# A gated merge on one core: banks given out by last read, sums finished early, new orders of the gate products, x read back in eight steps

## The chip, the core and the metric

The kernel runs on one core of a Trainium2 chip. The metric is the device time of one execution in microseconds. Engines: PE (matrix products, with PEld loading its weights), DVE (elementwise), ACT (copies, casts, activations), POOL, and SP (here it only issues DMAs). Each has a queue of its own and takes its instructions in order; they wait for one another by semaphores. PE writes into eight accumulator banks, each 128 x 512 in f32.

## The reference

One layer of a hybrid decoder on x of 256 x 2048, in f32. The part that the change touches:

```python
z = x @ mix_w_in[i]
b_gate, c_gate, h_conv, q_raw, f_raw, i_in, g_raw, gate_conv, gate_hgrn = jnp.split(z, splits, axis=-1)
y_conv = short_conv_mixer(b_gate, c_gate, h_conv, conv_w[i])
y_hgrn = hgrn2_mixer(q_raw, f_raw, i_in, g_raw, lower_bounds[i], hg_norm_w[i])
merged = (jax.nn.sigmoid(gate_conv) * (y_conv @ branch_w_conv[i])
          + jax.nn.sigmoid(gate_hgrn) * (y_hgrn @ branch_w_hgrn[i]))
x = layer_norm(ALPHA * x + merged @ mix_w_out[i], ln_g[i, 1], ln_b[i, 1])
```

gate_conv and gate_hgrn are 2048 columns each; y_conv and y_hgrn have 1024. Ahead of it stand a feed-forward block with its norm, behind it another one and a small gated embedding, each with a norm.

## The kernel before

**Stages.** lead1, ffn1, tail1, hgrn, **merge**, lead2, ffn2, tail2, ple. The merge stage holds the sigmoid gates, the two branch products and `merged @ mix_w_out`. The 256 rows of x are two tiles t = 0, 1 of 128 rows.

**Precision.** Every f32 product is three matmuls in a faster format: with w = wh + wl and x = xh + xl, L1149 does wh·xh, L1150 wl·xh, L1151 wh·xl (function `passes`). In the rows of PE, xh and xl (s, gh, gl) are the moving operand, 128 x 512 outputs.

**Weights.** Nothing of the weights stays on the core. Each piece (two K-tiles by 512 columns, 512 KB) goes SP's DMA into a buffer `raw` (L1022), ACT's cast to wh (L1082), DVE's split wl = raw - wh (L1093), PE. There are four raw buffers for plain pieces and small rings for the pieces of a Quad (in the rows below a number behind the name, raw_8548, marks such a one; plain pieces are just raw). A raw buffer is free when its split is done; wh and wl have six slots, in merge two more. `feed` issues loads, sums, casts and splits as far ahead as buffers let it; the compiler's scheduler may then move them within an engine's queue.

**A Quad** (`run_quad`) multiplies x by two blocks of 512 gate columns at once (the conv gate's and the hgrn gate's, columns c of 4) by a seven-product scheme: for half of K, 14 steps named 11, t1, 22, t3, t2, 21, t4 with .0 or .1 behind them, each six matmuls into one of the products p1 to p7; the steps t1 to t4 first need a sum of two weight pieces on DVE (L1061), the operands' sums exist already. For the other half of K, eight plain pieces a0 to a3 (conv gate) and u0 to u3 (hgrn gate) of 12 matmuls. In the merge, u's go into p3 (t = 0) and r (t = 1); r goes on in the bank of p1 when p1 has been copied out. The table `ORDER` says in what order the 22 pieces are taken. That makes 180 matmuls.

**Closing functions.** As products become complete, functions in `gate_units` read them: `first` (p1, copied), `second` (p3 copied, p5 added), `third` (p6, p7; and r and p5 once more), `fourth` (p2), `fifth` (p4, then sigmoids). `run_quad` calls one when all banks in its list are complete.

**Branch units.** Behind each Quad stand a Unit conv (y_conv by branch_w_conv) and a Unit hgrn (y_hgrn by branch_w_hgrn), 48 matmuls each, whose epilogues `epi_c` and `epi_h` multiply with the gates and add. I call a Quad with its two Units a pair of gate columns, 0 to 3. Then four units for mix_w_out.

**Banks.** `ptile` gives out the bank of its role whose `used_at` is lowest; `used` sets it. For gate Quads (`by_end`) each use by a matmul counts; otherwise the handing out counts.

**Deferred work.** `defer(n, fn)` runs fn n ticks later; a tick is six matmuls of a piece. In pair 3, `fifth` defers the transposes of the merged tiles m (`to_stat`, L283) and `load_stored` issues eight loads that bring x back from DRAM on POOL's queue (L372).

Of the kernel before, what the change touches and what calls it, by code (L numbers as in the profile page):

```python
# [14 lines left out]
ALU = mybir.AluOpType  # L15
# [5 lines left out]
NT = 2  # L21
DFF = 5504
CW = 1024
CC = 512
# [42 lines left out]
class Quad:  # L67
# [19 lines left out]
    ORDER = {  # L87
# [3 lines left out]
    }  # L91

    def __init__(self, stat, w, cols, width, after, form):
        self.stat, self.w, self.cols, self.width, self.after = stat, w, cols, width, after
        short = form == "short"
        self.shorted = not short
        self.by_end = form == "gate"
        order = self.ORDER[form].split()
        second = (("p3", 0), ("r", 1)) if form == "gate" else (("p3", "d"), ("p5", 1))
        made = {}  # L100


        for s, (lo, hi) in enumerate(self.STEPS):
            sums = (2 * s, 2 * s + 1)
            k11, k12, k21, k22 = ((self, s, n) for n in ("11", "12", "21", "22"))
            step = {
                "11": dict(src=k11, use=[("p1", 0, lo)], load=[(k11, lo, 0), (k22, hi, 1), (k12, lo, 1), (k21, hi, 0)]),
                "t1": dict(src=k11, add=(k11, k12), behind="11", use=[("p5", "s1", sums)]),
                "22": dict(src=k22, use=[("p3", "s4", sums)]),
                "t3": dict(src=k12, add=(k12, k22), behind="t1", use=[("p7", "s3", sums)], free=[k12]),  # L110
                "t2": dict(src=k11, add=(k11, k22), behind="t1 22", use=[("p6", "s2", sums)], drop=[k22]),
                "21": dict(src=k21, use=[("p2", 0, hi)]),
                "t4": dict(src=k11, add=(k11, k21), behind="t2 21", use=[("p4", 1, hi)], drop=[k21], free=[k11]),
            }
            for n, el in step.items():
                if "behind" in el:
                    el["behind"] = max(order.index(f"{m}.{s}") for m in el["behind"].split())
                made[f"{n}.{s}"] = el
        if short:
            made.update(self.short_step(order.index))  # L120
        for i, ks in enumerate(self.PLAIN):
            made[f"a{i}"] = dict(load=[(None, ks, 0)], use=[("p2", 0, ks), ("p4", 1, ks)])
            made[f"u{i}"] = dict(load=[(None, ks, 1)], use=[(*to, ks) for to in second])
        self.els = [made[n] for n in order]
# [17 lines left out]
def hybrid_layer(ctx: ExitStack, tc: tile.TileContext, x, p, ln_g, ln_b, ffn1_w_in, ffn1_w_out, mix_w_in,  # L142
                 conv_w, hg_lower_bound, hg_norm_w, branch_w_conv, branch_w_hgrn, mix_w_out,
                 ffn2_w_in, ffn2_w_out, ple_w_gate, ple_w_proj, out):
    nc = tc.nc
# [61 lines left out]
    gate = {}  # L207
# [159 lines left out]

    def load_stored():
        xt[:] = [res.tile([P, D], F32, tag=f"x{t}", name=f"x{t}") for t in range(NT)]
        for c in range(4):  # L370
            for t in range(NT):
                nc.gpsimd.dma_start(xt[t][:, c * CC : (c + 1) * CC], stored[t, c])  # L372

    def gate_sums():

# [130 lines left out]
    def ffn(name, xs, w_in, w_out, ln_i, nxt):  # L506
# [7 lines left out]
        def in_units(ch, g, ci):  # L514
            c0 = starts[ch]
            w = starts[ch + 1] - c0
            if ch > 1:
                made = {}

                def work(tag):  # L520
                    return st.tile([P, CC], F32, tag=tag, name=tag, bufs=2 if tag == "silu" else 3)

                def both(o, a, b, op):
                    nc.vector.tensor_tensor(out=o, in0=a, in1=b, op=op)

                def first(ps):
                    made["c11"] = work("h")
                    nc.scalar.copy(made["c11"], ps["p1"])

                def second(ps):  # L530
                    c = made["c12"] = work("silu")
                    nc.scalar.copy(c, ps["p3"])
                    both(c, c, ps["p5"], ALU.add)

                def third(ps):
                    e = made["e"] = work("silu")
                    made["c22"] = work("h")
                    with tc.issue_after(state["split"]):
                        both(e, made["c11"], ps["p6"], ALU.add)
                    both(made["c12"], made["c12"], e, ALU.subtract)  # L540
                    both(e, e, ps["p7"], ALU.add)
                    both(made["c22"], ps["p5"], e, ALU.subtract)

                def fourth(ps):
                    h = made["c11"]
                    both(h, h, ps["p2"], ALU.add)
                    nc.scalar.activation(h, h, AF.Silu)
                    both(h, h, made["c12"], ALU.mult)
                    turn(g, 0, ci, h, CC)

                def fifth(ps):
                    e = made["e"]
                    both(e, e, ps["p4"], ALU.add)
                    nc.scalar.activation(e, e, AF.Silu)
                    both(e, e, made["c22"], ALU.mult)
                    turn(g, 1, ci, e, CC)

                after = deque([(("p1",), first), (("p3", "p5"), second), (("p6", "p7"), third),
                               (("p2",), fourth), (("p4",), fifth)])
                units.append(Quad(xs, w_in, (c0, DFF + c0), CC, after, "short" if ch < 10 else "long"))  # L560
                return
            silu = {}

            def epi_a(t, acc):
                silu[t] = st.tile([P, CC], F32, tag="silu", name="silu", bufs=2)
                nc.scalar.activation(silu[t][:, :w], acc, AF.Silu)

            def epi_u(t, acc):
                h = st.tile([P, CC], F32, tag="h", name="h", bufs=3)
                nc.vector.tensor_tensor(out=h[:, :w], in0=silu[t][:, :w], in1=acc, op=ALU.mult)  # L570
                turn(g, t, ci, h, w)

            units.append(Unit(xs, w_in, 0, 16, c0, w, epi_a, split=(LONG if ln_i else EARLY) if ch == 0 else SPLIT))
            units.append(Unit(xs, w_in, 0, 16, DFF + c0, w, epi_u))
# [281 lines left out]
    def gate_units(c):  # L856
# [13 lines left out]
            nc.scalar.copy(made["conv", 0], ps["p1"])  # L870

        def second(ps):
            h = made["hgrn", 0] = work("silu")
            nc.scalar.copy(h, ps["p3"])
            both(h, h, ps["p5"], ALU.add)

        def third(ps):
            e = made["conv", 1] = work("silu")
            h = made["hgrn", 1] = work("h")
            with tc.issue_after(state["split"]):  # L880
                both(e, made["conv", 0], ps["p6"], ALU.add)
            both(made["hgrn", 0], made["hgrn", 0], e, ALU.subtract)
            both(e, e, ps["p7"], ALU.add)
            both(h, ps["p5"], e, ALU.subtract)
            both(h, h, ps["r"], ALU.add)

        def fourth(ps):
            both(made["conv", 0], made["conv", 0], ps["p2"], ALU.add)
# [2 lines left out]
        def fifth(ps):  # L891
            both(made["conv", 1], made["conv", 1], ps["p4"], ALU.add)
            for key in (("conv", 1), ("hgrn", 0), ("hgrn", 1)):
                sigmoid(made[key])
            if c == 3:
                share_banks({"a": 4, "t": 4})
                load_stored()
                for i in range(4):
                    defer(1 + 3 * i, lambda t=i % 2, cc=i // 2: to_stat(ms, t, cc, mc[t, cc], 4, "x"))

        def epi_c(t, acc):
            both(made["conv", t], made["conv", t], acc, ALU.mult)
# [3 lines left out]
        def epi_h(t, acc):  # L906
            m = mc[t, c] = made["conv", t] if c == 3 else rtile([P, CC], tag=f"m{t}{c}", name="m")
            both(made["hgrn", t], made["hgrn", t], acc, ALU.mult)
            both(m, made["conv", t], made["hgrn", t], ALU.add)
            if c == 3:  # L910
                defer(2, lambda: to_stat(ms, t, 3, m, 4, "g"))

        after = deque([(("p1",), first), (("p3", "p5"), second), (("p6", "p7"), third),
                       (("p2",), fourth), (("p4",), fifth)])
        cols = (7 * CW + c * CC, 7 * CW + D + c * CC)
        units.append(Quad(x1, wm, cols, CC, after, "gate"))
        units.append(Unit(ya, branch_w_conv[0], 0, 8, c * CC, CC, epi_c))
        units.append(Unit(yb, branch_w_hgrn[0], 0, 8, c * CC, CC, epi_h))

    mc = {}  # L920
# [250 lines left out]
    def run_quad(u, gi):  # L1171
# [5 lines left out]
        for el in u.els:  # L1177
            for i, (bank, t, ks) in enumerate(el["use"]):
                tick()
                first = bank not in ps  # L1180
                if first:
                    ps[bank] = ps["p1"] if bank == "r" else ptile("a", bank)
                if u.by_end:
                    used(ps[bank])
                for a, k in enumerate(ks):
                    left[bank] -= 1
                    passes(ps[bank], u.stat, t, k, gi, a if len(ks) > 1 else i, first and a == 0, left[bank] == 0)
            consumed(gi)
            while u.after and all(b in left and not left[b] for b in u.after[0][0]):
                u.after.popleft()[1](ps)  # L1190
            gi += 1
        return gi

# [44 lines left out]
```

## Time and profile before

| | us |
|---|---|
| three timed runs | 2236.07, 2236.68, 2237.87 (median 2236.68) |
| the profiled execution | 2239.12 |
| its span | 2237.4 |
| merge, first gate matmul behind the transposes to the last branch matmul | 1061.15 to 1334.40 |
| mean granted clock of the whole run | 0.992 of full |

Times in the rows are us from the start of the span, of one execution. A row of the timeline gives start, duration, engine, line, operation, out<-in and, in brackets, how long the engine was idle before and who released it. A row of waits gives the total, the number and the longest. "Loss" below means the time between starts of matmuls beyond what one takes when nothing waits.

### The profile page before, as it was taken

The page shows a single profiled execution, that of the slowest core. Times are in us where ns is not written, and L with a number is a line of the kernel's source. Part 1 is how long each engine was busy: PE and PEld are TensorE (multiplying, and loading weights), DVE is VectorE, ACT ScalarE, POOL GpSimd, SP SyncE. Part 2 cuts the span into 40 slices and gives each one's busy share as a digit, 9 for nine tenths or more (in the row PEclk, how much of TensorE's full clock was granted, in tenths as well). Part 3 has the DMA queues.
Part 4 walks back from the last instruction along what each step waited for, and adds up shares of the span by engine and source line. Part 5 has one row for each costly group of instructions (what it writes and reads, how often), then busy time and mean ns, then how long its engine had stood idle before and what let it go on. Part 6 is the DMA issues. An engine that isn't in the chain of part 4 may idle for free.

```text
span 2237.4 us, 27109 instructions
## 1 busy us (share of the span) xinstructions
PE 2197.3 (98%) x10038; PEld 1823.3 (81%) x10038; DVE 1809.1 (81%) x2046; ACT 1169.6 (52%) x1393; POOL 18.8 (1%) x48
## 2 busy tenths in 40 slices
PE   9999999999999999999999999999999999999997
PEld 7988888888877888888787778798888888888876
DVE  6799999999885578666878775679999999988668
ACT  5555555555555435533644453645555555556463
POOL 1000000000000000000000000000000000000000
PEclk9999999999999999999999999999999999999999
DMA  7666666666663655554755567465666666665564
GB/s 251 218 192 208 207 204 194 191 195 208 204 206 107 214 187 189 183 173 135 244 176 178 164 223 229 143 215 187 197 195 200 202 213 200 203 211 181 176 209 154
DMA packets 227129, 434.20 MB, mean 194 GB/s; under 512 B 14508, under 2 KB 23220, under 8 KB 226996
## 3 DMA queue, kind: packets, MB, share of 16 engines
q1 hardware_dynamic: 225716, 428.27, 60.1%
q0 software_dynamic: 1280, 4.20, 0.5%
q8 instruction: 78, 1.28, 0.2%
q14 instruction: 55, 0.45, 0.1%
HBM read 428.22 MB, written 4.19 MB: 193 GB/s over the span
## 4 chain that ended last, share of the span: by engine, by line
PE 90%; DVE 4%; DMA 3%; ACT 2%; issue 1%; DVEq 0%; SPq 0%; ACTq 0%
PE bank L1150 29%; PE bank L1149 29%; PE bank L1151 29%; DVE wl L1093 2%; PE bank L283 2%; ACT wh L1082 1%; DMA raw<-in_branch_w_hgrn_dram 1%; PE bank L698 1%; DMA raw<-in_ffn_w_in_dram 0%; DMA raw<-in_branch_w_conv_dram 0%; DMA raw<-in_mix_w_in_dram 0%; DVE raw L1061 0%; DVE x L499 0%; DVE x L500 0%; DMA raw<-in_ffn_w_out_dram 0%
## 5 line engine op out<-in xcount | busy, mean ns | idle before, releaser
L1082 ACT CAST wh<-raw 128x1024 fp32r<-128x1024 f32 (+1 forms) x968 | 969.3, 1031 | 824.3 <-PE bank L1151 405.9
L1093 DVE TENSOR_TENSOR wl<-raw,wh 128x1024 fp32r<-128x1024 f32 (+1 forms) x968 | 1135.1, 1199 | 272.2 <-ACT wh L1082 258.2
L1151 PE MATMUL bank<-wh,xl 128*128 128x512 f32 (+1 forms) x1672 | 647.4, 388 | 1.7 <-DVE xl L297 1.7
L1150 PE MATMUL bank<-wl,xh 128*128 128x512 f32 (+1 forms) x1672 | 647.9, 388 | 0.3 <-DVE wl L1093 0.3
L1149 PE MATMUL bank<-wh,xh 128*128 128x512 f32 (+1 forms) x1672 | 639.8, 390 | 4.5 <-ACT wh L1082 2.5
L1149 PEld LDWEIGHTS bank<-wh,xh 128*128 128x128 f32 x1672 | 315.9, 189 | 65.8 <-ACT wh L1082 3.3
L1151 PEld LDWEIGHTS bank<-wh,xl 128*128 128x128 f32 x1672 | 315.9, 189 | 63.0 <-DVE xl L297 2.3
L1150 PEld LDWEIGHTS bank<-wl,xh 128*128 128x128 f32 x1672 | 316.1, 189 | 60.5 <-DVE wl L1093 0.8
L1150 PE MATMUL bank<-wl,gh 128*128 128x512 f32 x896 | 350.7, 392 | 6.2 <-DVE wl L1093 5.9
L1149 PE MATMUL bank<-wh,gh 128*128 128x512 f32 x896 | 348.1, 394 | 6.1 <-ACT wh L1082 4.0
L1151 PE MATMUL bank<-wh,gl 128*128 128x512 f32 x896 | 349.0, 391 | 0.0
L1061 DVE TENSOR_TENSOR raw<-raw,raw 128x1024 f32<-128x1024 f32 x208 | 245.1, 1179 | 15.7 <-DMA raw<-in_ffn_w_in_dram 7.3
L1150 PEld LDWEIGHTS bank<-wl,gh 128*128 128x128 f32 x896 | 168.7, 188 | 45.5 <-DVE wl L1093 11.6
L1149 PEld LDWEIGHTS bank<-wh,gh 128*128 128x128 f32 x896 | 168.6, 188 | 45.5 <-ACT wh L1082 8.2
L1151 PEld LDWEIGHTS bank<-wh,gl 128*128 128x128 f32 x896 | 168.5, 188 | 34.5
L1150 PE MATMUL bank<-wl,sh 128*128 128x512 f32 x464 | 181.6, 391 | 0.0
L1151 PE MATMUL bank<-wh,sl 128*128 128x512 f32 x464 | 180.5, 389 | 0.0
L1149 PE MATMUL bank<-wh,sh 128*128 128x512 f32 x464 | 177.1, 389 | 0.0
L1149 PEld LDWEIGHTS bank<-wh,sh 128*128 128x128 f32 x464 | 87.1, 188 | 18.3
L1151 PEld LDWEIGHTS bank<-wh,sl 128*128 128x128 f32 x464 | 87.1, 188 | 17.9
L1150 PEld LDWEIGHTS bank<-wl,sh 128*128 128x128 f32 x464 | 87.1, 188 | 17.8
L296 ACT CAST gh<-bank 128x512 fp32r<-128x512 f32 (+2 forms) x54 | 30.7, 570 | 76.1 <-PE bank L283 75.5
(178 smaller groups left out, 1039.1 us busy)
## 6 DMA issues: line engine op xcount, KB each, us to landing
raw<-in_ffn_w_in_dram SPq DMA_DIRECT2D x288, 512.0 KB, 4.2
raw<-in_mix_w_in_dram SPq DMA_DIRECT2D x176, 512.0 KB, 4.7
raw<-in_ffn_w_out_dram SPq DMA_DIRECT2D x168, 512.0 KB, 4.8
raw<-in_ffn_w_in_dram SPq DMA_DIRECT2D x64, 256.0 KB, 3.0
raw<-in_mix_w_out_dram SPq DMA_DIRECT2D x32, 512.0 KB, 5.4
raw<-in_ple_w_gate_dram SPq DMA_DIRECT2D x32, 512.0 KB, 5.0
raw<-in_ffn_w_in_dram SPq DMA_DIRECT2D x32, 384.0 KB, 3.8
raw<-in_branch_w_conv_dram SPq DMA_DIRECT2D x16, 512.0 KB, 4.9
```

What stands on the lines that cost most here:

```text
L283: state["turned"] = nc.tensor.transpose(tp[:, i * P : (i + 1) * P], src[:, i * P : (i + 1) * P], ident).ins
L296: nc.scalar.copy(hf, src)
L698: nc.tensor.matmul(gp[:, (h * 2 + t) * 64 : (h * 2 + t + 1) * 64], kd[:, h, t * P : (t + 1) * P], qd[:, h, t, :], start=True, stop=True)
L1061: nc.vector.tensor_tensor(out=out, in0=a, in1=b, op=ALU.add)
L1082: nc.scalar.copy(h[:, :n, :w], raw[:, :n, :w])
L1093: state["split"] = nc.vector.tensor_tensor(out=l[:, :n, :w], in0=raw[:, :n, :w], in1=h[:, :n, :w].bitcast(F32), op=ALU.subtract).ins
L1149: nc.tensor.matmul(acc, sh, wh[:, a, :n], start=first, stop=False)
L1150: nc.tensor.matmul(acc, sh, wl[:, a, :n], start=False, stop=False)
L1151: nc.tensor.matmul(acc, sl, wh[:, a, :n], start=False, stop=last)
```

## The change

- `by_end` goes. A closing function now names the banks that it reads, and these count as used once the function has run.
- `second` waits for p3, p5 and r, and does copy and add for both tiles; `third` no longer computes the hgrn gate of tile 1 from r and p5. ACT has one copy more per Quad, DVE the same number of operations.
- The first Quad has an order of its own, `gate0`, that begins with four plain pieces; `gate` takes plain pieces a place or two earlier.
- `load_stored` defers its eight loads to ticks 2, 8, 14, and so on, and alternates the tiles. The transposes of m are deferred by other numbers of ticks.

```diff
-        "gate": "a0 11.0 a1 11.1 a2 t1.0 u0 22.0 t3.0 u1 t2.0 21.0 u2 t4.0 t1.1 u3 22.1 t3.1 a3 t2.1 21.1 t4.1",
+        "gate0": "a0 a1 a2 a3 11.0 11.1 t1.0 u0 22.0 t3.0 u1 t2.0 21.0 u2 t4.0 t1.1 u3 22.1 t3.1 t2.1 21.1 t4.1",
+        "gate": "a0 11.0 a1 11.1 a2 u0 t1.0 22.0 u1 t3.0 t2.0 u2 21.0 t4.0 u3 t1.1 22.1 a3 t3.1 t2.1 21.1 t4.1",
...
-        self.by_end = form == "gate"
...
-        for c in range(4):
-            for t in range(NT):
+        for i in range(8):
+            def load(t=i % 2, c=i // 2):
                 nc.gpsimd.dma_start(xt[t][:, c * CC : (c + 1) * CC], stored[t, c])
+
+            defer(2 + 6 * i, load)
...
         def second(ps):
-            h = made["hgrn", 0] = work("silu")
-            nc.scalar.copy(h, ps["p3"])
-            both(h, h, ps["p5"], ALU.add)
+            for t, bank in enumerate(("p3", "r")):
+                h = made["hgrn", t] = work("h" if t else "silu")
+                nc.scalar.copy(h, ps[bank])
+                both(h, h, ps["p5"], ALU.add)
 
         def third(ps):
             e = made["conv", 1] = work("silu")
-            h = made["hgrn", 1] = work("h")
             with tc.issue_after(state["split"]):
                 both(e, made["conv", 0], ps["p6"], ALU.add)
             both(made["hgrn", 0], made["hgrn", 0], e, ALU.subtract)
             both(e, e, ps["p7"], ALU.add)
-            both(h, ps["p5"], e, ALU.subtract)
-            both(h, h, ps["r"], ALU.add)
+            both(made["hgrn", 1], made["hgrn", 1], e, ALU.subtract)
...
-                    defer(1 + 3 * i, lambda t=i % 2, cc=i // 2: to_stat(ms, t, cc, mc[t, cc], 4, "x"))
+                    defer(2 + 3 * i, lambda t=i % 2, cc=i // 2: to_stat(ms, t, cc, mc[t, cc], 4, "x"))
...
-                defer(2, lambda: to_stat(ms, t, 3, m, 4, "g"))
-
-        after = deque([(("p1",), first), (("p3", "p5"), second), (("p6", "p7"), third),
-                       (("p2",), fourth), (("p4",), fifth)])
+                defer(5 - t, lambda: to_stat(ms, t, 3, m, 4, "g"))
+
+        after = deque([(("p1",), first, ("p1",)), (("p3", "p5", "r"), second, ("p5", "r", "p3")),
+                       (("p6", "p7"), third, ("p6", "p7")), (("p2",), fourth, ("p2",)), (("p4",), fifth, ("p4",))])
...
-        units.append(Quad(x1, wm, cols, CC, after, "gate"))
+        units.append(Quad(x1, wm, cols, CC, after, "gate" if c else "gate0"))
...
-                if u.by_end:
-                    used(ps[bank])
...
             while u.after and all(b in left and not left[b] for b in u.after[0][0]):
-                u.after.popleft()[1](ps)
+                _, fn, read = u.after.popleft()
+                fn(ps)
+                for b in read:
+                    used(ps[b])
```

**ACT at the start of the merge, before.** gh<-bank is the operand of the hgrn branch, b and gh<-z belong to the conv branch (z is a product on DVE that needs PE's transposes of b). The last four rows are the casts of 11.0, a1, 11.1 and a2.

```order
L296 CAST gh<-bank_83 128x512
L735 ACTIVATE junk,ss<-bank_82 128x128 x4
L429 ACTIVATE r<-w 128x4
L834 COPY b<-bank_85 128x512
L296 CAST gh<-bank_87 128x512
L296 CAST gh<-z 128x512
L834 COPY b<-bank_86 128x512
L296 CAST gh<-z 128x512
L1082 CAST wh<-raw_8548 128x1024
L1082 CAST wh<-raw 128x1024
L1082 CAST wh<-raw_8550 128x1024
L1082 CAST wh<-raw 128x1024
```

The same place after:

```order
L296 CAST gh<-bank_83 128x512
L737 ACTIVATE junk,ss<-bank_82 128x128 x4
L1083 CAST wh<-raw 128x1024
L431 ACTIVATE r<-w 128x4
L836 COPY b<-bank_85 128x512
L1083 CAST wh<-raw 128x1024 x2
L296 CAST gh<-bank_87 128x512
L836 COPY b<-bank_86 128x512
L296 CAST gh<-z 128x512 x2
L1083 CAST wh<-raw_8566 128x1024
L1083 CAST wh<-raw_8568 128x1024
L1083 CAST wh<-raw_8566 128x1024
```

Behind r<-w there is now a plain cast (a1), then two more (a2, a3) ahead of gh<-bank_87; the pieces with numbers, 11.0 and 11.1, come behind gh<-z.

**PE at the end of pair 0, before.** The first five rows end step t4.1 (bank 3); gh_7062 is the first half of y_hgrn's operand of tile 0.

```order
L1150 MATMUL bank3_84<-wl_8815,xh_5864 128x512
L1151 MATMUL bank3_84<-wh_8814,xl_5865 128x512
L1149 MATMUL bank3_84<-wh_8814,xh_5864 128x512
L1150 MATMUL bank3_84<-wl_8815,xh_5864 128x512
L1151 MATMUL bank3_84<-wh_8814,xl_5865 128x512
L1149 MATMUL bank5_86<-wh_8877,gh_7062 128x512
L1150 MATMUL bank5_86<-wl_8878,gh_7062 128x512
L1151 MATMUL bank5_86<-wh_8877,gl_7063 128x512
L1149 MATMUL bank5_86<-wh_8877,gh_7062 128x512
L1150 MATMUL bank5_86<-wl_8878,gh_7062 128x512
```

The same place after; gh_7192 and gh_7240 are y_conv's operands of the two tiles:

```order
L1150 MATMUL bank3_84<-wh_8814,xh_5864 128x512
L1150 MATMUL bank4_85<-wh_8832,gh_7240 128x512
L1150 MATMUL bank0_81<-wh_8832,gh_7192 128x512
L1151 MATMUL bank3_84<-wl_8815,xh_5864 128x512
L1152 MATMUL bank3_84<-wh_8814,xl_5865 128x512
L1150 MATMUL bank3_84<-wh_8814,xh_5864 128x512
L1151 MATMUL bank3_84<-wl_8815,xh_5864 128x512
L1152 MATMUL bank3_84<-wh_8814,xl_5865 128x512
L1151 MATMUL bank0_81<-wl_8833,gh_7192 128x512
L1152 MATMUL bank0_81<-wh_8832,gl_7193 128x512
L1150 MATMUL bank0_81<-wh_8832,gh_7192 128x512
```

Before, the hgrn unit follows t4.1, and conv comes 42 rows later; after, conv does, in banks 0 and 4. In pairs 1 and 2 the same is seen. On POOL nothing moves: the eight loads x<-stored stand in one block, four of tile 0, then four of tile 1, before and after. SP's row has the loads of branch_w_conv a little earlier among the gate's; outside the merge only the numbers of banks differ.

More of the change, by code (lines that the diff above doesn't have):

```diff
@@ L96, in __init__ @@
         self.shorted = not short
-        self.by_end = form == "gate"
         order = self.ORDER[form].split()
-        second = (("p3", 0), ("r", 1)) if form == "gate" else (("p3", "d"), ("p5", 1))
+        second = (("p3", 0), ("r", 1)) if form[:4] == "gate" else (("p3", "d"), ("p5", 1))
         made = {}
@@ L556, in fifth @@
                     turn(g, 1, ci, e, CC)
-                after = deque([(("p1",), first), (("p3", "p5"), second), (("p6", "p7"), third),
-                               (("p2",), fourth), (("p4",), fifth)])
+                after = deque([(("p1",), first, ()), (("p3", "p5"), second, ()), (("p6", "p7"), third, ()),
+                               (("p2",), fourth, ()), (("p4",), fifth, ())])
                 units.append(Quad(xs, w_in, (c0, DFF + c0), CC, after, "short" if ch < 10 else "long"))
@@ L910, in epi_h @@
             if c == 3:
-                defer(2, lambda: to_stat(ms, t, 3, m, 4, "g"))
-        after = deque([(("p1",), first), (("p3", "p5"), second), (("p6", "p7"), third),
-                       (("p2",), fourth), (("p4",), fifth)])
+                defer(5 - t, lambda: to_stat(ms, t, 3, m, 4, "g"))
+        after = deque([(("p1",), first, ("p1",)), (("p3", "p5", "r"), second, ("p5", "r", "p3")),
+                       (("p6", "p7"), third, ("p6", "p7")), (("p2",), fourth, ("p2",)), (("p4",), fifth, ("p4",))])
         cols = (7 * CW + c * CC, 7 * CW + D + c * CC)
-        units.append(Quad(x1, wm, cols, CC, after, "gate"))
+        units.append(Quad(x1, wm, cols, CC, after, "gate" if c else "gate0"))
         units.append(Unit(ya, branch_w_conv[0], 0, 8, c * CC, CC, epi_c))
```

## The prediction

> **What bounds the kernel now.** I read the page first, then PE's waits, then busy time by stretch, then single rows.
>
> ```profile
> span 2237.4 us, 27109 instructions
> PE 2197.3 (98%) x10038; PEld 1823.3 (81%) x10038; DVE 1809.1 (81%) x2046; ACT 1169.6 (52%) x1393; POOL 18.8 (1%) x48
> PE 90%; DVE 4%; DMA 3%; ACT 2%; issue 1%; DVEq 0%; SPq 0%; ACTq 0%
> ```
>
> PE is busy 98% of the span and carries 90% of the chain that ended last. The change removes no matmul, so all it can win is time in which PE stands still or runs below its clock. The merge stage (1061 to 1334 us) is the only one in which the order of work differs. I cut it into its eight parts: for each of the four pairs of gate columns the gate product (a Quad, 180 matmuls), then the branch units conv and hgrn (96 matmuls). Columns: us; busy time and instructions of PE, PEld, DVE, ACT, POOL; granted clock; DMA share; GB/s.
>
> ```profile
> 1061.15:1105.33 44.18, 41.66 (x168) 33.47 (x168) 39.99 (x37) 27.65 (x29) 0.00 (x0) 0.92 0.70 227
> 1105.33:1132.56 27.23, 24.42 (x98) 18.97 (x98) 19.51 (x21) 12.71 (x14) 0.00 (x0) 0.94 0.56 175
> 1132.56:1173.46 40.90, 40.90 (x181) 33.79 (x180) 33.94 (x33) 21.89 (x23) 0.00 (x0) 1.00 0.62 203
> 1173.46:1199.02 25.56, 23.22 (x97) 17.70 (x96) 18.00 (x21) 10.55 (x12) 0.00 (x0) 1.00 0.50 162
> 1199.02:1239.93 40.91, 40.91 (x182) 33.79 (x180) 35.10 (x34) 23.71 (x25) 0.00 (x0) 1.00 0.63 202
> 1239.93:1266.10 26.17, 23.08 (x97) 17.78 (x96) 19.31 (x21) 11.33 (x13) 0.00 (x0) 1.00 0.54 174
> 1266.10:1307.03 40.93, 40.93 (x182) 33.79 (x180) 34.66 (x33) 22.25 (x24) 2.48 (x5) 1.00 0.46 144
> 1307.03:1334.40 27.37, 25.30 (x122) 20.25 (x121) 19.75 (x25) 15.12 (x20) 1.85 (x4) 1.00 0.75 265
> ```
>
> Rows 3, 5 and 7 give the price of a matmul when nothing waits: 40.9 us / 180 = 0.227 us. With it, each other row has a loss:
> - row 1 (pair 0's Quad; 168 matmuls, since 12 were issued before): 44.18 - 168 x 0.227 = 6.0 us
> - rows 2, 4 and 6 (branch units, 96 x 0.227 = 21.8): 5.4, 3.7 and 4.4 us
> - row 8: 21.8 plus 24 transposes at 0.14 (below, eight take 1.12 us from their start to the next matmul's, 3.4 in all), so 2.2 us.
>
> Sum **21.7 us**, 1.0% of the span. That is all that there is to win here. PE's waits in this stretch say for whom it stands (total us, times, longest):
>
> ```profile
> PE bank L1150 <- DVE wl L1093: 5.6, 8, 0.8
> PE bank L1149 <- ACT wh L1082: 5.1, 5, 2.4
> PE bank L283 <- DVE sig L860: 1.5, 1, 1.5
> PE bank L1149 <- DVE sig L860: 0.6, 1, 0.6
> ```
>
> That is 12.8 us of the 21.7, nearly all for a weight's cast or split. The rest is matmuls at half clock:
>
> ```profile
> 1059.81:1063.22 3.41, 1.34 (x8) 0.89 (x7) 1.35 (x2) 1.31 (x2) 0.00 (x0) 1.00 0.11 16
> 1063.22:1070.05 6.83, 6.38 (x14) 4.71 (x15) 6.57 (x7) 6.03 (x7) 0.00 (x0) 0.50 0.85 300
> 1107.60:1111.01 3.41, 1.36 (x5) 0.58 (x4) 1.71 (x2) 2.09 (x2) 0.00 (x0) 1.00 0.98 359
> 1111.01:1114.42 3.41, 3.41 (x10) 2.35 (x9) 3.41 (x5) 3.25 (x4) 0.00 (x0) 0.50 0.81 214
> 1175.86:1179.27 3.41, 2.32 (x8) 1.41 (x9) 3.19 (x4) 2.08 (x3) 0.00 (x0) 1.00 0.80 268
> ```
>
> Both half-clock stretches follow a stretch of 3.41 us in which PE was busy 1.34 or 1.36 us; one with 2.32 busy was followed by none. So short waits that lie close together cost twice, and go twice.
>
> **Part 1: the merge's start (6.0 us).**
>
> ```profile
> 1060.55 0.60 PE L283 MATMUL bank<-ident,b 128*128 128x128 f32 x4
> 1061.91 0.62 ACT L296 CAST gh<-z 128x512 fp32r<-128x512 f32 x1 [3.32 <-DVE z L840]
> 1062.43 3.88 ACT L1082 CAST wh<-raw 128x1024 fp32r<-128x1024 f32 x4
> 1063.52 0.80 PE L1149 MATMUL bank<-wh,xh 128*128 128x512 f32 x1 [2.38 <-ACT wh L1082]
> ```
>
> After a0's matmuls and the transposes of b, PE waits 2.38 us for a cast. ACT was idle 3.32 us for z (which needs those transposes) with the casts queued behind gh; then four elements' casts and splits follow one another while PE, now at half clock, eats them as they come. In the new order the casts of a1, a2, a3 stand ahead of that gh, and PE has a0 to a3, 48 matmuls = 10.9 us, with the transposes of b in their middle. ACT's wait stays but is covered: from the first of those transposes to the first matmul of 11.0 it is 63.52 - 60.55 = 3.0 us, and 26 of the 48 matmuls, 5.9 us, stand behind them. I take 5.5 of the 6.0 here; if the casts still stood behind gh, none.
>
> **Part 2: the branch units of pairs 0 to 2 (13.5 us).**
>
> ```profile
> 1106.59 0.50 PE L1150 MATMUL bank<-wl,gh 128*128 128x512 f32 x1 [0.75 <-DVE wl L1093]
> 1108.22 1.04 ACT L1082 CAST wh<-raw 128x1024 fp32r<-128x1024 f32 x1 [2.94 <-DMA raw<-in_branch_w_hgrn_dram]
> 1109.32 0.50 PE L1149 MATMUL bank<-wh,gh 128*128 128x512 f32 x1 [1.29 <-ACT wh L1082]
> ```
>
> The kernel's text puts conv first, then hgrn, and loads in that order; but PE's row has hgrn right behind t4.1 (order rows above). Conv's accumulator is p5's bank, which `third` still has to read. So PE asks first for the weights that land last, and waits for cast and split one by one. Now a bank ages by its last read; conv gets the banks of p5 and p1/r, whose readers (`second`) run early, and PE takes conv first. hgrn comes 48 matmuls = 10.9 us later. The waits seen here reach 1.29 us each and total 2.8 in pair 0: cover of four times that. A hoisted cast of a late conv weight still blocks ACT for a DMA, but now ahead of matmuls that have their weights. I take 12.5 of the 13.5, with 0.3 left in pairs 1 and 2 together and the rest in pair 0 (below).
>
> **Part 3: pair 3 (2.2 us).**
>
> ```profile
> 1304.55 4.33 POOL L372 DMA_DIRECT2D x<-stored  x8 [328.31 <-PE bank L1151]
> 1313.04 1.05 ACT L1082 CAST wh<-raw 128x1024 fp32r<-128x1024 f32 x1 [5.12 <-DMA raw<-in_branch_w_hgrn_dram]
> 1315.27 0.69 DVE L860 TENSOR_TENSOR sig<-sig 128x512 f32<-128x512 f32 x1
> 1316.60 1.36 PE L283 MATMUL bank<-ident,m 128*128 128x128 f32 x8 [1.45 <-DVE sig L860]
> raw<-in_branch_w_hgrn_dram SPq DMA_DIRECT2D x2, 512.0 KB, 9.3
> ```
>
> x comes back in one burst at 1304.55, beside which a weight takes 9.3 us to land (last row, the DMA issues of 1304 to 1320). DVE waits for that weight's split with the product for m queued behind it, and the transpose of m waits 1.45. The text now spreads the eight loads over ticks, but POOL's row is the same eight in one block, of which only the first of each tile waits: **the burst stays**. The transposes are put off by a few ticks. They still need a bank whose reader stands behind a split of an hgrn weight. I take 1.2 of the 2.2: half the wait gone, 0.57 of the other wait too.
>
> **Part 4: sums.** Four more copies on ACT, nothing more on DVE:
>
> ```profile
> L874 ACT COPY sig<-bank x4: 572/574/576, 1100.5 to 1301.6; 128x512 f32<-128x512 f32 x4
> L860 DVE TENSOR_TENSOR sig<-sig,bank x40: 676/680/690, 1102.2 to 1336.9; 128x512 f32<-128x512 f32 x40
> raw<-in_branch_w_conv_dram SPq DMA_DIRECT2D x16, 512.0 KB, 4.9
> ```
>
> 4 x 0.574 = 2.3 us of an ACT that is busy 22 of 41 us in a Quad. `second` now waits for p5 and r too, and behind its copies ACT has the cast of t4.1 and of conv's first weight. All three sums are complete with step 22.1; PE then still has a3, t3.1, t2.1 and 21.1, 30 matmuls = 6.8 us, before it needs t4.1. So 0; without that cover 2.3, and nothing to gain on ACT. The late weight's cast, hoisted to stand ahead of t1.1, waits for a load that follows the split of u2; ACT passes 21.0, t4.0 and u3 meanwhile, 24 matmuls = 5.4 us at PE's pace, against 4.9 for such a load (last row). Taken at 0, at worst some 1 us a pair; it belongs to the slower rival.
>
> **Sum.** 5.5 + 12.5 + 1.2 = 19.2, less 0.3 for what I can't place: **18.9 us**. The profiled execution took 2239.12, so 2220.2 of that kind; the three timed runs have a median of 2236.68, so 2217.8. Outside the merge only bank numbers differ.
>
> **The rivals.**
>
> *Pair 0 runs out of DVE.* In row 1 DVE is busy 39.99 us. Unstalled, the Quad takes 38.2. The splits of a1 to a3 (3 x 1.2) move ahead of it, so 36.4 of 38.2 remain: it fits, barely. If it doesn't, PE waits there for splits, and hgrn's first cast comes late as now: pair 0 keeps the branch's 5.4 and the 3.5 of the 6.0 that aren't the first wait. Then 8.9 more stays, less the 1.0 which I left there: 11 won, **2226**. Speaks for it: saturation; against: the order gives DVE 48 matmuls' lead at the start.
>
> *The clock loss isn't due to these waits.* Of the 21.7 us, 12.8 are waits; 8.9 are slow or late matmuls, about 6 of them in the two half-clock stretches. If those came anyway, 12.9 would be won: **2224**. The trace speaks against it: each stretch stands right behind a starved one.
> The Trainium skill, "TensorE: Matmul & The Clock Gate", "Part 1: The HAM clock gate" and "Why this matters for your kernels", has the half rate begin after an idle window of about 3.4 us, and asks for no gaps over about 3 us. The longest gap here is 2.38 us, and windows with 1.34 busy were enough: by the page these waits would not have cost the clock, by the rows they did.
>
> *The banks aren't why PE takes hgrn first*, or the order on the chip undoes it: only the start is won, 6.0: **2231**. PE's new row speaks against it.
>
> *Slower: DVE falls behind in each Quad's end.*
>
> ```profile
> L1093 DVE TENSOR_TENSOR wl<-raw,wh 128x1024 fp32r<-128x1024 f32 (+1 forms) x968 | 1135.1, 1199 | 272.2 <-ACT wh L1082 258.2
> L1061 DVE TENSOR_TENSOR raw<-raw,raw 128x1024 f32<-128x1024 f32 x208 | 245.1, 1179 | 15.7 <-DMA raw<-in_ffn_w_in_dram 7.3
> ```
>
> From t1.1 on, the new "gate" has 7 splits (8.4), 4 sums of weights (4.7) and about six adds (4.1) on DVE: 17.2 us, against 48 matmuls, 10.9 us. The 6.3 us must come from lead; the old tail, with u3 in it, had one split (1.2) and 12 matmuls (2.7) more, so 4.8, and shows no wait (rows 3, 5, 7). It decides where DVE's lead at t1.1 is under 6.3 us: without any, four times 6.3 plus 1.7 for a half-clock stretch each, 32 us, against 18.9 won: **2250**; break-even at 3.3 us of lead. The 4.8 already covered speak against it.
>
> **How the numbers follow.** Forecast 2218 (2215, all 21.7 won, to 2222): 0.62. Pair 0's DVE, 2226: 0.17. Clock stays, 2224: 0.08. Start alone, 2231: 0.08. Slower, 2240 to 2250: 0.05. The range must leave out no more than 0.2; with the 4 copies or a small gain unaccounted at the lower end it is 2213 to 2229, which leaves out the last two and a little. A measurement of this kernel tells 0.2%, 4.5 us, from no change: faster means under 2232.2. Of the start-alone case half lies above that; so faster 0.89, same 0.06, slower 0.05.
>
> **What would show it.** Part 1: no PE gap over 0.5 us and full clock from 1060 to 1070, pair 0's Quad in 38 to 40 us. Part 2: branch stretches of 22 to 22.5 us with no wait for an hgrn cast, clock 1.00. Part 3: x still one block of 4.3 us on POOL, one wait of under 1 us ahead of a transpose of m. Part 4: ACT busy 0.6 us more per Quad, Quads 1 to 3 still 40.9. It is wrong if PE waits in Quads 1 to 3 (the slower rival), or if pair 0's DVE is above 97% busy and PE waits for wl there.

## The result, and the profile after

| | before | changed |
|---|---|---|
| timed runs, median (lowest to highest), us | 2237.27 (2236.07 to 2237.87) | 2215.83 (2215.76 to 2215.93) |
| ratio, 95% interval | | 0.9899 (0.9884 to 0.9913) |
| profiled execution: time, span | 2239.12, 2237.4 | 2215.93, 2214.2 |

The gain is 21.4 us by the medians, against 18.9 forecast. The page of the changed kernel (busy time per engine, then the chain that ended last):

```profile
span 2214.2 us, 27113 instructions
PE 2187.6 (99%) x10038; PEld 1821.3 (82%) x10038; DVE 1808.0 (82%) x2046; ACT 1171.8 (53%) x1397; POOL 19.0 (1%) x48
PE 92%; DVE 4%; DMA 1%; ACT 1%; issue 1%; SPq 0%; DVEq 0%; ACTq 0%
```

PE has as many instructions as before and is busy 9.7 us less (2197.3 before): at half clock a matmul counts as busy for longer, and so do the matmuls next to a wait (sizes in the section on why the prediction was right). The merge by parts, as before (us; PE, PEld, DVE, ACT, POOL busy; granted clock; DMA share; GB/s). The first row begins behind the second transposes of b, 1062.40; before, that place was 1061.15. Between the first two rows lie 1.59 us, with the first two matmuls of conv and the last five of t4.1.

```profile
1062.40:1097.41 35.01, 35.01 (x156) 28.81 (x155) 33.58 (x32) 23.09 (x26) 0.00 (x0) 1.00 0.66 217
1099.00:1120.52 21.52, 21.52 (x96) 17.83 (x95) 18.55 (x22) 13.79 (x15) 0.00 (x0) 1.00 0.76 243
1120.52:1161.21 40.69, 40.69 (x180) 33.60 (x179) 37.04 (x34) 23.01 (x24) 0.00 (x0) 1.00 0.66 211
1161.21:1183.00 21.79, 21.79 (x98) 18.04 (x97) 16.91 (x20) 10.57 (x12) 0.00 (x0) 1.00 0.60 185
1183.00:1223.88 40.88, 40.88 (x182) 33.76 (x180) 33.72 (x31) 23.95 (x25) 0.00 (x0) 1.00 0.58 186
1223.88:1245.64 21.76, 21.76 (x98) 18.02 (x96) 19.75 (x23) 11.34 (x13) 0.00 (x0) 1.00 0.72 230
1245.64:1286.55 40.91, 40.91 (x182) 33.79 (x181) 34.65 (x32) 22.47 (x24) 2.49 (x5) 1.00 0.49 146
1286.55:1311.19 24.64, 24.64 (x121) 20.33 (x120) 20.73 (x26) 15.72 (x21) 1.84 (x4) 1.00 0.84 291
```

In every row PE's busy time is the whole stretch, and the clock is 1.00. The branch stretches take 21.5 to 21.8 us instead of 25.6 to 27.2; the Quads of pairs 1 to 3 are unchanged within 0.2 us. The view of PE's waits from 1045 to 1315 is empty.

What has not gone is ACT's wait for hgrn's weights. ACT's timeline at the end of pair 0, changed:

```profile
1099.75 1.05 ACT L1083 CAST wh<-raw 128x1024 fp32r<-128x1024 f32 x1 [1.80 <-DMA raw<-in_branch_w_hgrn_dram]
1104.54 1.05 ACT L1083 CAST wh<-raw 128x1024 fp32r<-128x1024 f32 x1 [3.74 <-DMA raw<-in_branch_w_hgrn_dram]
```

Before, the second of these waits was 2.94 us. It is longer now and costs nothing, since PE has conv's matmuls meanwhile. The same holds at the merge's start: ACT waits for z longer than before (3.32 us there), but behind casts that are done.

```profile
1063.40 0.62 ACT L296 CAST gh<-z 128x512 fp32r<-128x512 f32 x1 [5.04 <-DVE z L842]
```

To place the gain I compared the start times of the same PE instruction, by number, in two traces. Outside the merge the profiles differ by 0.7 us; within it the changed kernel is 22.5 us shorter. This is the measure of the table below.

### The profile page after: what moved, and what is told of

Its sections match the earlier page's. It is cut to its first block, busy times and chain, and to the rows that moved or that the text cites. A ratio compares the mean times of both kernels' runs of the same rounds, so it can differ in the third digit from the quotient of the medians.

```text
span 2214.2 us, 27113 instructions
## 1 busy us (share of the span) xinstructions
PE 2187.6 (99%) x10038; PEld 1821.3 (82%) x10038; DVE 1808.0 (82%) x2046; ACT 1171.8 (53%) x1397; POOL 19.0 (1%) x48
## 4 chain that ended last, share of the span: by engine, by line
PE 92%; DVE 4%; DMA 1%; ACT 1%; issue 1%; SPq 0%; DVEq 0%; ACTq 0%
PE bank L1150 30%; PE bank L1151 30%; PE bank L1152 29%; PE bank L283 2%; DVE wl L1094 2%; PE bank L700 1%; ACT wh L1083 1%; DVE raw L1062 1%; DMA raw<-in_ffn_w_out_dram 1%; DMA raw<-in_ffn_w_in_dram 0%; DVE silu L526 0%; DVE x L501 0%; DMA x<-in_x_dram 0%; DVE x L502 0%; DMA raw<-in_ple_w_gate_dram 0%
```

## The experiments

Theory, as predicted: (1) the start is starved because casts stand behind gh; (2) in pairs 0 to 2 PE meets the unit whose weights land last, since conv's bank still has to be read, and the ageing by last read mends that; (3) x in eight steps does nothing. Main rivals: either half of the bank edit suffices; the new order of pairs 1 to 3 matters; the parts don't add. All kernels compute the same values, in other orders.

**The new order of pair 0 alone** (e_start, on the kernel before):

```diff
+        "gate0": "a0 a1 a2 a3 11.0 11.1 t1.0 u0 22.0 t3.0 u1 t2.0 21.0 u2 t4.0 t1.1 u3 22.1 t3.1 t2.1 21.1 t4.1",
...
-        self.by_end = form == "gate"
+        self.by_end = form[:4] == "gate"
...
-        second = (("p3", 0), ("r", 1)) if form == "gate" else (("p3", "d"), ("p5", 1))
+        second = (("p3", 0), ("r", 1)) if form[:4] == "gate" else (("p3", "d"), ("p5", 1))
...
-        units.append(Quad(x1, wm, cols, CC, after, "gate"))
+        units.append(Quad(x1, wm, cols, CC, after, "gate" if c else "gate0"))
```

> The kernel before with the new order gate0 in pair 0 alone; banks, sums, the order of pairs 1 to 3, x and the delays are those of before. Theory (the start is starved because casts stand behind gh): the 6.0 us at the merge's start go, the four branch stretches keep their 5.4, 3.7, 4.4 and 2.2 us: about 2231. Rival (the plain pieces at the front also let the branch weights of pair 0 load earlier): pair 0's 5.4 goes too, 2226. Rival (the sums of weights come late instead): 2235 or more.

**All but that order** (e_nostart, on the changed kernel):

```diff
-        units.append(Quad(x1, wm, cols, CC, after, "gate" if c else "gate0"))
+        units.append(Quad(x1, wm, cols, CC, after, "gate"))
```

> The changed kernel with gate instead of gate0 in pair 0; all else as changed. Theory: the 6 us at the start come back, with a half-clock stretch behind a gap of over 2 us, and nothing else: about 2222. Rival (gate0 is needed for DVE's lead in the rest of pair 0): 2226.

**Both edits of the banks, the early sums alone, the ageing alone** (e_banks, e_sums, e_age, on the kernel before). e_banks has the sums and the ageing as in the change's diff. e_sums has the change's second and third, and of the rest only this:

```diff
-        after = deque([(("p1",), first), (("p3", "p5"), second), (("p6", "p7"), third),
+        after = deque([(("p1",), first), (("p3", "p5", "r"), second), (("p6", "p7"), third),
```

e_age has the change's lines in run_quad, with second and third as before, so that third is the last to read p5 and r (the Quads of the feed-forward block get empty lists and go on as before):

```diff
-        after = deque([(("p1",), first), (("p3", "p5"), second), (("p6", "p7"), third),
-                       (("p2",), fourth), (("p4",), fifth)])
+        after = deque([(("p1",), first, ("p1",)), (("p3", "p5"), second, ("p3",)),
+                       (("p6", "p7"), third, ("p6", "p7", "p5", "r")), (("p2",), fourth, ("p2",)), (("p4",), fifth, ("p4",))])
```

> The kernel before with the banks given out by last read and with p5 and r summed in second; orders, x and delays as before. Theory (conv first is what saves the branch stretches): 13.5 us less in pairs 0 to 2 and about 1 in pair 3, the start's 6 stay: about 2222. Rival (the new order gate, which loads the last plain piece earlier, is needed as well): a branch stretch keeps half of its loss, about 2229.

> The kernel before with p5 and r summed in second and nothing else: banks still age by each use, orders, x and delays as before. Its row of PE has conv ahead of hgrn, like that of the changed kernel. Theory as predicted (the ageing by last read is what puts conv first): no gain, 2237. Rival (the early sums free conv's banks by themselves): as with both, about 2222.

> The kernel before with the banks given out by last read and nothing else: third still reads p5 and r, orders, x and delays as before. Its row of PE also has conv first, in banks other than p5's. Theory after the first four runs (conv first is what counts, and either of the two edits gives it): the branch stretches of pairs 0 to 2 lose nothing, the start keeps its 3.4 to 6, pair 3 some 1 to 4: 2219 to 2223, as the sums alone. Rival (ageing alone is only half of it, since units then wait for third's reads of p5 and r): a wait for DVE's sums at each pair's end, 2227 or more.

**The changed kernel with one part undone**: the order of pairs 1 to 3 (e_oldgate), x and the delays (e_xold), the ageing (e_byend).

```diff
-        "gate": "a0 11.0 a1 11.1 a2 u0 t1.0 22.0 u1 t3.0 t2.0 u2 21.0 t4.0 u3 t1.1 22.1 a3 t3.1 t2.1 21.1 t4.1",
+        "gate": "a0 11.0 a1 11.1 a2 t1.0 u0 22.0 t3.0 u1 t2.0 21.0 u2 t4.0 t1.1 u3 22.1 t3.1 a3 t2.1 21.1 t4.1",
```

> The changed kernel with the order gate of before in pairs 1 to 3. Theory (the order of pairs 1 to 3 does not matter once conv is first): within 1 us of the changed kernel, 2216, no wait of PE in pairs 0 to 2. Rival (taking u and a pieces earlier is what brings the late branch weights in time): 1 to 2 us of waits for casts or splits in each of pairs 1 to 3, 2219 to 2222.

```diff
-                    defer(2 + 3 * i, lambda t=i % 2, cc=i // 2: to_stat(ms, t, cc, mc[t, cc], 4, "x"))
+                    defer(1 + 3 * i, lambda t=i % 2, cc=i // 2: to_stat(ms, t, cc, mc[t, cc], 4, "x"))
...
-                defer(5 - t, lambda: to_stat(ms, t, 3, m, 4, "g"))
+                defer(2, lambda: to_stat(ms, t, 3, m, 4, "g"))
...
-        for i in range(8):
-            def load(t=i % 2, c=i // 2):
+        for c in range(4):
+            for t in range(NT):
                 nc.gpsimd.dma_start(xt[t][:, c * CC : (c + 1) * CC], stored[t, c])
-
-            defer(2 + 6 * i, load)
```

The old loop takes the tiles in turn as the new one does; only the deferring differs.

> The changed kernel with the loads of x in one loop and with the delays of the transposes of m as before. POOL's row is the same in both. Theory as predicted (x in eight steps changes nothing, the delays spare about 1 us in pair 3): 2216 to 2217, with one wait of 1 to 1.7 us ahead of a transpose of m. Rival (the delays are worth all of the pair's 2.2 to 2.7, with a half-clock stretch if the window falls so): 2218 to 2220. Rival (nothing): 2215.8.

```diff
+        self.gate = form[:4] == "gate"
...
+                if u.gate:
+                    used(ps[bank])
...
-                for b in read:
-                    used(ps[b])
```

> The changed kernel with banks ageing by each use of a matmul again; sums, orders, x and delays as changed. Theory after the first four runs (the early sums suffice): 2216, no wait in pairs 0 to 2. Theory as predicted (ageing by last read is needed): the branch stretches lose again, 2225 or more. Third: only pair 3, where transposes take turns in the banks, loses 1 to 3 us, 2217 to 2219.

**Two edits alone** (f_min: e_start's and e_sums' together, on the kernel before).

> The kernel before with two edits: gate0 in pair 0, and p5 and r summed in second. No ageing by last read, the order gate, x and the delays as before. Theory (the start needs casts ahead of gh, the branch stretches need conv first, and the sums alone give that): the start and pairs 0 to 2 lose nothing, pair 3 loses 1 to 4 us: 2216 to 2219. Rival (each part of the change carries a share): 2220 or more.

**One plain piece ahead instead of three** (f_one, on the changed kernel):

```diff
-        "gate0": "a0 a1 a2 a3 11.0 11.1 t1.0 ...
+        "gate0": "a0 a1 11.0 a2 11.1 a3 t1.0 ...
```

> The changed kernel with one plain piece more ahead in pair 0 instead of three: a0 a1 11.0 a2 11.1 a3. Theory (what counts is the matmuls that cover the 3.0 us from the transposes of b to the first matmul of 11.0): a1 is 2.7 us, but some of it lies ahead of the transposes, so a wait of 0.5 to 2 us stays, with or without half clock: 2216.5 to 2219. Rival (three pieces are needed, DVE's lead being what counts): as with none, 2219 or more.

**The units exchanged** (f_swap, on the kernel before, in pairs 0 to 2; the sum is formed in the second unit's epilogue):

```diff
+        if c < 3:
+            units.append(Unit(yb, branch_w_hgrn[0], 0, 8, c * CC, CC, epi_h0))
+            units.append(Unit(ya, branch_w_conv[0], 0, 8, c * CC, CC, epi_c1))
...
```

> The kernel before with the hgrn unit ahead of the conv unit in the text of pairs 0 to 2, so that branch_w_hgrn is loaded first; the same arithmetic. In PE's row it is again the second unit, now conv, that follows the Quad. Theory (PE meets the unit whose weights land last, whichever it is, because the first unit's bank is still to be read): the branch stretches lose the same 3.5 to 5.5 us each, now waiting for branch_w_conv: 2235 to 2241. Rival (something about hgrn's weights or operands is slow): 2222 to 2226.

**The kernel before, profiled again** (f_before_again).

> The kernel before, unchanged, profiled a second time. Theory (half clock comes after a stretch of a free-running grid of 3.41 us in which PE was busy less than about 1.9 us, so the same waits cost more or less with the grid's phase): PE's waits in the merge are the same 12.8 us within 0.3, but the half-clock stretches stand behind other waits. Rival (half clock belongs to fixed places): the same two stretches, at the merge's start and in pair 0.

**What was measured.** The loss columns are us by which a stretch of PE instructions in the profile is longer than in the changed kernel: the start with the first half of pair 0's Quad, the rest of pair 0, pairs 1, 2 and 3. Medians and ratios are of the timed runs, ratios to the kernel before on the same chip. On the three chips of the experiments its medians were 2238.87, 2239.25 and 2240.23.

| kernel | start | pair 0 | 1 | 2 | 3 | median us | ratio (95%) |
|---|---|---|---|---|---|---|---|
| before | 6.0 | 5.5 | 3.8 | 4.4 | 2.7 | 2237.27 | |
| before, again | 3.4 | 8.1 | 4.4 | 3.9 | 3.9 | 2238.86, one run | |
| f_swap | 3.4 | 7.7 | 5.0 | 5.6 | 3.6 | 2238.95 | 0.9996 (0.9988 to 1.0005) |
| e_start | 0.0 | 7.8 | 4.9 | 3.5 | 6.6 | 2236.65 | 0.9983 (0.9973 to 0.9993) |
| e_age | 6.0 | -0.1 | 0.0 | 0.0 | 1.1 | 2222.01 | 0.9929 (0.9916 to 0.9943) |
| e_sums | 5.0 | -0.1 | 0.0 | 0.0 | 3.1 | 2221.21 | 0.9915 (0.9901 to 0.9930) |
| e_banks | 5.1 | -0.1 | 0.0 | 0.0 | 0.9 | 2219.79 | 0.9908 (0.9894 to 0.9922) |
| e_nostart | 3.4 | -0.1 | 0.0 | 0.0 | 0.0 | 2218.96 | 0.9909 (0.9894 to 0.9923) |
| f_one | 4.5 | 0.1 | 0.0 | 0.0 | 0.0 | 2219.99 | 0.9911 (0.9896 to 0.9926) |
| f_min | 0.0 | 0.1 | 0.0 | 0.0 | 2.4 | 2218.32 | 0.9905 (0.9891 to 0.9919) |
| e_oldgate | 0.0 | 0.0 | 0.0 | 0.0 | 0.9 | 2215.20 | 0.9895 (0.9881 to 0.9908) |
| e_byend | 0.0 | 0.0 | 0.0 | 0.0 | -0.1 | 2216.56 | 0.9901 (0.9887 to 0.9914) |
| e_xold | 0.0 | 0.0 | 0.0 | 0.0 | 0.0 | 2214.95 | 0.9895 (0.9881 to 0.9908) |

Each row of columns is one profile. Where nothing is lost the columns agree within 0.1 us; the size of a loss changes from profile to profile (the first two rows are one kernel). The intervals of the ratios tell less: the changed kernel's is 0.9884 to 0.9913, and of the kernels with a bank edit only e_age's lies clear of it. The last three kernels are not shown to beat the changed one.

*Branch stretches.* The sums alone and the ageing alone each take the whole of pairs 0 to 2, and without the ageing the changed kernel loses nothing there. PE's waits in the merge, in e_sums and then in e_age, are those at the start and ahead of the transposes of m (1045 to 1325):

```profile
PE bank L1148 <- ACT wh L1081: 2.8, 2, 2.4
PE bank L283 <- DVE sig L860: 2.8, 2, 1.5
```

```profile
PE bank L1148 <- ACT wh L1081: 2.5, 2, 2.4
PE bank L282 <- DVE sig L859: 0.7, 1, 0.7
```

The order of the program's instructions says why. With the sums alone conv still gets p5's bank (bank 0 for one tile of pair 0), but that has been read when PE comes to it. With the ageing alone, p5's bank counts as used late, by third, and conv gets two other banks. In both, PE has conv directly behind t4.1. The trace of e_sums bears this out: PE is in pair 0's branch units from 1100.93 and waits for nothing, though hgrn's second weight is cast only at 1106.12. f_swap settles that it is no matter of hgrn: with hgrn first in the text, conv, now second, follows the Quad and is waited for. ACT's timeline in f_swap at the end of pair 0, and the matmul that waits for the first of these casts:

```profile
1103.88 1.04 ACT L1094 CAST wh<-raw 128x1024 fp32r<-128x1024 f32 x1 [1.38 <-DMA raw<-in_branch_w_conv_dram]
1107.48 1.04 ACT L1094 CAST wh<-raw 128x1024 fp32r<-128x1024 f32 x1 [2.55 <-DMA raw<-in_branch_w_conv_dram]
1104.98 0.49 PE L1161 MATMUL bank<-wh,gh 128*128 128x512 f32 x1 [2.89 <-ACT wh L1094]
```

*Start.* Without gate0, PE's waits in the merge are the two at its start and no others (e_nostart, 1050 to 1325):

```profile
PE bank L1150 <- ACT wh L1083: 2.8, 2, 2.4
```

I had expected 6 us and a half-clock stretch. The loss is 3.4 us, and full clock goes on: in the stretch of the grid with this wait PE is still busy 1.74 us.

f_one sizes the cover. Its PE timeline shows that only two matmuls of a1 lie behind the transposes of b; two of 0.227 us are 0.45, and the wait of 2.38 is shorter by that:

```profile
1062.45 0.60 PE L283 MATMUL bank<-ident,b 128*128 128x128 f32 x4
1062.81 0.47 PE L1151 MATMUL bank<-wl,xh 128*128 128x512 f32 x1
1063.12 0.39 PE L1152 MATMUL bank<-wh,xl 128*128 128x512 f32 x1
1065.43 0.49 PE L1150 MATMUL bank<-wh,xh 128*128 128x512 f32 x1 [1.92 <-ACT wh L1083]
```

Pieces ahead count only from the transposes on. My expectation (2216.5 to 2219) took more of a1 to lie there. The time, 2219.99, falls where the rival put it, that three pieces are needed for DVE's lead; but PE waits for casts here and for no split of DVE. A half-clock stretch follows the shorter wait, so one piece ahead cost as much in this profile as none, or more (4.5 against 3.4).

*Parts don't add.* gate0 by itself takes the start's whole loss. I had expected 2231; the median is 2236.65, and the time falls by 0.17% (0.07 to 0.27%), where 6.0 us would be 0.27%. That lies in the range of the rival by which the sums of weights come late, but PE waits for nothing from 1050 to 1099. It comes to pair 0's end earlier and meets the same late weights (PE timeline, e_start):

```profile
1100.05 0.50 PE L1150 MATMUL bank<-wh,gh 128*128 128x512 f32 x1 [2.16 <-ACT wh L1083]
1101.31 0.50 PE L1151 MATMUL bank<-wl,gh 128*128 128x512 f32 x1 [0.76 <-DVE wl L1094]
```

That stretch loses 7.8 us where the first profile of before lost 5.5, but 8.1 in the second, whose start lost less. Pair 3 loses 6.6 in e_start, with a wait of 2.5 us ahead of a transpose and 6.83 us of half clock. In sum its columns lose 22.8 us, as much as those of before (22.4 and 23.7). That a later wait takes back what the start wins fits this, but one profile doesn't show how much of it is the place of the grid. With conv first, gate0 is worth 3.4 us in the profile of e_nostart.

*Pair 3.* With the old order, the sums alone leave 3.1 (f_min 2.4) and the ageing takes it to 0.9 (e_banks); the new order gate takes that as well, with the ageing or without it, with the new delays or the old. The order without an edit of the banks was not run, and why it spares the wait is not shown. In e_oldgate, from 1045 to 1315, one wait for DVE stays:

```profile
PE bank L283 <- DVE sig L862: 0.7, 1, 0.7
```

*Half clock.* The second profile of before is the one that tells most (columns as above):

```profile
1058.79:1062.20 3.41, 2.19 (x12) 1.62 (x10) 0.69 (x1) 0.46 (x1) 0.00 (x0) 1.00 0.00 0
1062.20:1065.62 3.42, 1.82 (x7) 1.30 (x8) 2.97 (x3) 3.42 (x5) 0.00 (x0) 1.00 0.81 258
1103.16:1106.58 3.42, 0.49 (x1) 0.19 (x1) 3.35 (x4) 1.23 (x2) 0.00 (x0) 1.00 0.93 274
1106.58:1109.99 3.41, 2.89 (x6) 1.78 (x6) 1.19 (x3) 1.22 (x2) 0.00 (x0) 0.50 1.00 368
1174.84:1178.25 3.41, 1.60 (x6) 0.86 (x5) 2.05 (x3) 2.14 (x3) 0.00 (x0) 1.00 0.89 317
1178.25:1181.66 3.41, 3.41 (x9) 2.60 (x8) 3.41 (x5) 2.22 (x3) 0.00 (x0) 0.50 0.80 228
```

The same wait at the start (2.38 us before) is split here between two stretches of the grid, neither starved enough, and full clock goes on. Half clock follows in pair 0, elsewhere than in the first profile, and in pairs 1 and 3, which had kept full clock there. The places move, so the rival of fixed places falls. Its waits total 13.5 us (7.5 for casts, 4.0 for splits, 2.0 for a transpose) against 12.8, not the same within 0.3 as expected.

## Why the prediction was right

- *Bound by PE, 21.7 us to win.* Right: 22.5 us of the merge went, and nothing else moved by more than 0.7. The bound was 0.8 short, mostly in pair 3 (2.7, not 2.2): where nothing waits, row 8 takes 24.64 us, which leaves 2.8 for its 24 transposes, not 3.4. "The rest is matmuls at half clock" is too simple. PE was busy 9.79 us in the two half-clock stretches; matmuls started every 0.43 us there instead of 0.227, so I estimate that full clock would have saved 4.6 us. The other 4 to 5 us lie next to the waits: a matmul ahead of one counts as busy for 0.39 us, where the next usually starts after 0.227, and behind one the next started after 0.33 (1110.58 to 1110.91).
- *Part 1, 5.5 of 6.0.* All 6.0 went, and by the cover that was named: ACT's wait is 5.04 us behind the casts of a1 to a3. But the 6.0 was the loss of one profile; in another it was 3.4 (before, again). As a part alone it was worth 0.17%.
- *Part 2, 12.5 of 13.5.* All of it went (5.5 + 3.8 + 4.4 = 13.7 in the table). That conv first is the cause is shown by e_sums, e_age and f_swap. **The step that failed** is "Now a bank ages by its last read; conv gets the banks of p5 and p1/r": the ageing isn't needed. I took two edits for one mechanism; either frees a bank for conv in time.
- *Part 3, 1.2 of 2.2.* Mis-sized: all of it went, and the wait ahead of a transpose that I expected to stay is not there. I looked for the gain in the delays, and they give nothing: e_xold waits nowhere, where I had expected 1 to 1.7 us, and with the old order 0.9 stays with the new delays (e_oldgate) as with the old (e_banks). With the early sums the order gate takes all of it (e_byend), and the ageing a part. x in one block on POOL was right, 4.33 us as before:

```profile
1284.06 4.33 POOL L372 DMA_DIRECT2D x<-stored  x8 [308.54 <-PE bank L1152]
```

- *Part 4, 0.* Right: ACT is busy 2.2 us more in all (1171.8 against 1169.6), and PE waits for none of it.
- *The sum, 18.9 against 21.4.* What I held back, 1.0 in Part 2, 1.0 in Part 3 and 0.8 otherwise, wasn't lost. That the parts come out so close is in part luck: I took their sizes from one profile, and the second one of the same kernel has 3.4 for 6.0 and 8.1 for 5.5. The failed step didn't show in the time, because the change has both edits.
- *Rival: pair 0 runs out of DVE.* DVE is busy 33.58 of the 35.01 us of the first row after, 96%, as close as worked out, and PE waits for none of it.
- *Rival: the clock loss isn't due to the waits.* Falls: where the waits are gone, the clock is 1.00 in all eight rows. The Trainium skill, "TensorE: Matmul & The Clock Gate", "Why this matters for your kernels", asks for no gaps over about 3 us. It doesn't say that shorter ones are safe, as the prediction read it, and here they weren't: in f_one two gaps of 1.92 and 0.45 us were followed by a half-clock stretch.

```profile
1062.98:1066.39 3.41, 1.03 (x5) 0.30 (x3) 2.36 (x3) 2.58 (x4) 0.00 (x0) 1.00 0.41 98
1066.39:1069.80 3.41, 3.41 (x8) 2.74 (x9) 3.41 (x4) 2.60 (x3) 0.00 (x0) 0.50 1.01 379
```

- *Rival: the banks aren't why PE takes hgrn first.* Falls: either edit of the banks alone puts conv first, and e_start, which has neither, keeps 7.8, 4.9 and 3.5 us in pairs 0 to 2.
- *Rival: slower by DVE in the Quads' ends.* Falls: 40.69, 40.88 and 40.91 us, and no wait.

## What to carry to other kernels

Where a matrix engine waits for a weight, ask first why it came to that weight so early: a unit that was written first can be held back by a buffer that someone still has to read, and the next unit, whose data come last, takes its place. A wait needn't be removed if other work can stand ahead of it; count that work from the instruction that the wait depends on. Test the halves of a change one by one: two edits that each free the same resource look like one mechanism, and gains at one place can be given back at the next wait.

## What the runs showed of the hardware

- The half clock is granted on a grid of 3.41 us, which lies elsewhere in each profile. In the first one of before the two half-clock stretches begin at 1063.22 and 1111.01, and 47.79 us are 14 times 3.41. What counted was PE's busy time in a stretch, not the length of one gap. In the merge stages of these 14 profiles a full-clock stretch with PE busy 1.67 us or less was followed by half clock each time (14 such stretches), one with 1.85 or more never; between these both occurred (1.79 was in e_sums; 1.74 in e_nostart and 1.82 above were not). The border is not sharp elsewhere either: at about 701 us stretches with 1.86 (e_age), 1.90 (before) and 1.92 (f_one) were followed by half clock, and one with 1.92 (e_oldgate) was not. In the merge a half-clock stretch was the last where PE was busy 3.05 us or more in it, and after 2.02 to 2.93 a second one followed; of two between, 2.95 (f_before_again) was the last and 2.96 (before) was not. So the same gap of 2.38 us cost 3.4 us at the merge's start in one profile and 6.0 in another.
- The kernel before scatters more than the changed one: in the runs of the result, 2236.07 to 2237.87 against 2215.76 to 2215.93, four each; on another chip before took 2236.43 to 2246.49 in 17 runs. That starved stretches meet the grid by chance would explain a part; no run tests this, and four runs of e_byend, whose profile has no wait of PE in the merge, lie between 2215.22 and 2218.01.
- ACT's waits grew while the kernel got faster: 5.04 and 3.74 us in the changed kernel, against 3.32 and 2.94.
